# More seven-product pairs in a hybrid attention and SSM block, with weight sums and left factors made ahead

## The chip, the cores and the metric

The kernel runs on one core of one Trainium2 chip. The metric is the device time in microseconds of one execution; lower is better. Every run is a whole execution of the block on its fixed inputs.

## The reference, cut to what matters

One layer takes x (256 rows of 2048) through a norm and one wide product with `w_in`. From that come attention's q, k, v and gate, the SSM's inputs and gate, and two gates of the output. The attention and the SSM results go through one weight matrix each, are gated, added, and go through `w_out`; the input is added and a last norm follows. All is float32.

```
proj = rms_norm(x) @ w_in
q, k, v, z_a, z_s, xbc, dt_raw, g_a, g_s = split(proj)
o_a = attention(q, k, v) * silu(z_a)                 # 16 heads of 128
y = rms_norm(ssd_scan(xbc, dt_raw) * silu(z_s))      # 4096 wide
merged = sigmoid(g_a) * (o_a @ w_attn_branch) + sigmoid(g_s) * (y @ w_ssm_branch)
return rms_norm(x + merged @ w_out)
```

## The kernel before

**Precision.** Each float32 operand of a product is held as two parts, a high part h (type `fp32r`) and a low part l, the rest. ScalarE (ACT) makes h by a copy, VectorE (DVE) makes l by a subtraction. A product is then three matmuls: h with h, h with l, l with h. A "triple" in the code is these three.

**Weights.** All weights lie in one array `wall` of units of 128 x 1024 values (512 KB), in the order in which they are used (`weight_plan`). One unit is loaded by SyncE's DMA queue (SP) into a ring of four buffers w, converted into one of four buffers h and l (`unit`), and used. The conversions are given priority by 120 places (`L_AHEAD`); a scheduler that works with a timeline of its own sets the order of the instructions on every engine, and which of the ring's buffers a load gets.

**Stages**, in order: a first product; the SSM stage, eight groups that project four pairs of xs and zs column blocks each (`project`, `gemm_a`), with convolution, decay, scan and the transposed result `yT` of 32 kt (a kt is 128 rows of the contraction); two pairs ("ssm", 0) and ("ssm", 2) for the SSM branch's 2048 columns; pairs ("v", 0), ("v", 2) and ("ga", 2); attention, 16 heads of q, k and z_a projections with scores, softmax (`scores`), transposed p (`turn_p`) and `mix`; ("ga", 0) and ("ga", 1) by `gates`; the attention branch: pair ("attn", 0), then columns 2 and 3 by `gemm_b`; and pairs ("out", 0), ("out", 2).

**Two ways for a wide product.** `gemm_b` (through `gates`, too) makes 512 columns: per kt and half of the rows one triple, so per two kt and 1024 columns 2 x 2 x 2 x 3 = 24 matmuls of 128x512. `gemm_pair` makes 1024 columns at once. It goes in steps q of two kt. A plain step is again 24 matmuls. A step listed in `S_QUADS` is a quad: the 2 x 2 x 2 block products are made from seven products instead of eight (Strassen's scheme in Winograd's form), so 21 matmuls. A quad needs sums of its four weight blocks and of its four left blocks:

- `t13` and two differences of weights, made by DVE when the weights have come (L432, L437, L438), split into high and low parts `ha, la`, `hc, lc`, and, in two buffers of their own, `ht, lt` and `hu, lu` (L425, L426);
- left factors `sx`, made by `turn_x` from the transposed left matrix: one addition of 128x512 (L355) and four additions or subtractions of 128x128 (L357 to L360), then splits (L230 on ACT, L232 on DVE).

Four extra accumulators `prods` collect products that several outputs share; `fold` adds them at the end.

**Order in time.** Small work is queued with `after(ticks, f)`; a tick is one projection or one step of two kt. `on_unit[n]` runs a function when unit n is converted; `fetch` then lets GpSimd (POOL) copy one column of that unit's h into the target, which makes the DMA behind it wait until then. SP serves its DMAs in their order, and a wait holds up what stands behind it.

Of the kernel before, what the change touches and what calls it, by code (L numbers as in the profile page):

```python
# [15 lines left out]
P = 128  # L16
# [15 lines left out]
MUL_PAD = 112  # L32
# [3 lines left out]
DT_LAG, CB_LAG, TURN_LAG, GT_LAG, Y_LAG, S_LAG, M_LAG = 2, 5, 3, 2, 11, 2, 2  # L36
GS_BEFORE = {0: (0, 1), 4: (2,)}
# [18 lines left out]
def weight_plan():  # L56
# [50 lines left out]
def lay_weights(mats):  # L107
    out = np.empty((N_UNITS, P, UNIT), np.float32)
    for tag, form, src, off, n_kt, w in PLAN:
# [6 lines left out]
        if form == "p":  # L116


            m = m.reshape(n // 2, 2, P, 2, 512)
            for q in range(n // 2):  # L120
                f = FIRST[tag] + 2 * q
                if q in S_QUADS[tag]:
                    out[f] = np.concatenate([m[q, 0, :, 0], m[q, 1, :, 1]], axis=1)
                    out[f + 1] = np.concatenate([m[q, 0, :, 1], m[q, 1, :, 0]], axis=1)
                else:
                    out[f : f + 2] = m[q].reshape(2, P, UNIT)
            continue
# [45 lines left out]
def hybrid_block(ctx: ExitStack, tc: tile.TileContext, wall, xt, x, pk_d, cst_d, fw_d, out):  # L173
# [15 lines left out]
    lead.tile([P, 8], F32, name="fill", tag="fill")  # L189
# [15 lines left out]
    on_unit = {}  # L205

# [6 lines left out]
    def unit(n, shape):  # L213
# [10 lines left out]
        if n in on_unit:  # L224
            on_unit.pop(n)(h[:, 0:1].bitcast(F32))
# [3 lines left out]
    def split(src, hi, lo, scale=1.0):  # L229
        ac.activation(hi, src, AF.Copy, scale=scale)  # L230
        if isinstance(scale, float):
            ve.tensor_tensor(lo, src, hi.bitcast(F32), ALU.subtract)  # L232
        else:
            ve.scalar_tensor_tensor(lo, src, scale, hi.bitcast(F32), ALU.mult, ALU.subtract)

# [35 lines left out]
    def gemm_dt(src):  # L271
# [8 lines left out]
        for u, tag in enumerate("hl"):  # L280
# [4 lines left out]
            if n in on_unit:  # L285
                on_unit.pop(n)(hl[:, 0, 0, 0:1].bitcast(F32))
            ve.tensor_tensor(hl[:, :, 1], w[:, ks], hl[:, :, 0].bitcast(F32), ALU.subtract)
            for kk in range(half_kt):
                kt = u * half_kt + kk
                pe.matmul(  # L290
                    acc, hl[:, kk].rearrange("p n m -> p (n m)"), src[:, kt, :], start=(kt == 0), stop=(kt == KT - 1)
# [6 lines left out]
    def gemm_first(tag, prepare, load_on):  # L298
        name = f"{tag[0]}{tag[1]}"
        accs = [bank("g", 4, f"ps_{name}_{j}") for j in range(4)]  # L300
        for u in range(KT // UB):
# [6 lines left out]
            for kk in range(UB):  # L308
                kt = u * UB + kk
                m = yT[0][:, kt, :]  # L310
# [37 lines left out]
    def turn_x(pool, bufs, temp, x, spare=0):  # L348


        sx = pool.tile([P, 2, 4 - spare, P], F32R, name=f"sx{now[0]}", tag="sx", bufs=bufs)
# [9 lines left out]
        parts = [(sx[:, 0, n], sx[:, 1, n]) for n in range(4 - spare)]  # L361
        if spare:
            own = x[:, 0, P:S], x[:, 0, S + P :]
            split(s[:, 0], *own)
            parts.insert(0, own)
        split(s[:, spare:], sx[:, 0], sx[:, 1])
        return parts

    def gemm_pair(tag, x_of, n_kt, sxs, swap, extra={}, close=1):
# [20 lines left out]
        for q in range(n_q):  # L390
            tick()
            if q in extra:
                extra[q]()
# [3 lines left out]
            if q not in quads:  # L397
                ready = [] if q <= n_q - close else ready
                ready += [(a, k, *unit(n + k, (2, 512))) for k in range(2)]
                if n_q - close <= q < n_q - 1:  # L400
                    continue
                steps = [(e, i, c) for e in ready for i in range(2) for c in range(2)]
                if q == n_q - 1:
                    steps.sort(key=lambda s: s[1:])
                for e, i, c in steps:
# [3 lines left out]
                        start=(q == 0 and k == 0), stop=(q == n_q - 1 and e is ready[-1]),  # L409
# [19 lines left out]
            with tc.high_priority(L_AHEAD):  # L429
                t13 = mul.tile([P, UNIT], F32, name=f"t13_{n}", tag="t13", bufs=1)  # L430
                b12 = wb[:, :512].unsqueeze(1).to_broadcast([P, 2, 512])
                ve.tensor_tensor(two(t13), b12, two(wa), ALU.subtract)  # L432
# [4 lines left out]
                ve.tensor_tensor(wb[:, :512], wa[:, 512:], t13[:, :512], ALU.subtract)  # L437
                ve.tensor_tensor(wb[:, 512:], wb[:, 512:], wb[:, :512], ALU.subtract)  # L438
                ht, lt = hl(mul, "t", ("ht", "lt"), 2)
                part(t13, ht, lt)  # L440
                hu, lu = hl(mul, "u", ("ht", "lt"), 2)
                part(wb, hu, lu)
            sx = sxs[q]
            lo, hi = slice(0, 512), slice(512, 1024)
            go, end = q == quads[0], q == quads[-1]
            for acc, x, h, l, cs, own in (
                (prods[0], a[0][0], ha, la, lo, True),
                (es[1], sx[3], ha, la, hi, False),
                (es[0], a[0][1], hc, lc, lo, False),
                (prods[1], sx[0], ht, lt, lo, True),  # L450
                (prods[3], sx[1], ht, lt, hi, True),
                (prods[2], sx[2], hu, lu, lo, True),
# [16 lines left out]
    def gates(tag, th, src, scales=(0.5, 0.5)):  # L469
        accs = gemm_b(tag, lambda kt: src[:, kt, :])  # L470
# [3 lines left out]
    def rsqrt_rows(sums, n, name):  # L474
# [4 lines left out]
        hr = cpool.tile([P, 2], F32, name=f"hr_{name}", tag="hr", bufs=2)  # L479
# [12 lines left out]
    early = big.tile([P, 29, S], F32, name="early", tag="yo1")  # L492
    xr, dts, rx = early[:, :KT, :], early[:SH, KT:28, :], early[:, 28, :]
    yT = [big.tile([P, KT, 2 * S], F32R, name="yT0", tag="yo0")]
# [15 lines left out]
    def split_x(kt):  # L510
        split(xr[:, kt], yT[0][:, kt, :S], yT[0][:, kt, S:], scale=pk[:, kt : kt + 1])
# [18 lines left out]
    for n in range(4):  # L530
        on_unit[6 + n] = lambda behind, n=n: fetch_x(n, behind)
    on_unit[10] = lambda behind: fetch(cst[:, 1152:], cst_d[:, 1152:], behind)
    on_unit[13] = lambda behind: fetch(cst[:, :1152], cst_d[:, :1152], behind)
# [20 lines left out]
    with tc.tile_pool(name="ssm", bufs=2) as sp:  # L554
# [9 lines left out]
        sp.tile([P, 8], F32, name="line_s", tag="line", bufs=1)  # L564
# [114 lines left out]
        def scan(g, state):  # L679
# [11 lines left out]
            for v, yp in enumerate(yps):  # L691
                u = 2 * g + v
                xs, zs = state["xs"][v], state["zs"][v]
# [9 lines left out]
                if u == 8:  # L703
                    yT.append(big.tile([P, KT, 2 * S], F32R, name="yT1", tag="yo1"))
                dst = yT[u // 8]
                for i in range(2):
                    t = 2 * u + i
                    split(y1[:, i], dst[:, t % 16, :S], dst[:, t % 16, S:], scale=nw[:, t : t + 1])
# [17 lines left out]
        dt_sum(gemm_dt(yT[0]))  # L726
# [18 lines left out]
        for c, u in RX_UNITS.items():  # L745
            on_unit[u] = lambda behind, c=c: (later_rx(c)(behind), norm_x(c))
# [9 lines left out]
        for c in GS_BEFORE[0]:  # L756
            gates(("gs", c), th_s, yT[0], hr_x)

        for g in range(GROUPS):
# [9 lines left out]
            for t in range(max(4 * g, 1), 4 * g + 4):  # L769
# [4 lines left out]
                if t % 4 == 3:  # L774
# [6 lines left out]
                    after(y_lag, lambda a=(g, state): scan(*a), 1)  # L781
                conv(collect(acc, f"x{t}"), t, state["xs"][-1][:, i], f"x{t}")
# [11 lines left out]
    mul.tile([P, MUL_PAD], F32, name="line", tag="line")  # L794
# [13 lines left out]
    def blocks(t, c):  # L808
        return [t[:, i, (c + j) * 512 : (c + j + 1) * 512] for i in range(2) for j in range(2)]

    def two_kts(t, q):
        return t[:, 2 * q : 2 * q + 2, :]

    with tc.tile_pool(name="xp", bufs=1) as xp:
        sxs = {}
        for c in (0, 2):
            for q in S_QUADS[("ssm", c)]:
                if q not in sxs:
                    temp = xp.tile([P, 4, 512], F32, name=f"sxt_y{q}", tag="tmp", bufs=1)
                    sxs[q] = turn_x(xp, 6, temp, two_kts(yT[q // 8], q % 8), 1)  # L820
            es, prods = gemm_pair(
                ("ssm", c), lambda kt: yT[kt // 16][:, kt % 16, :], 2 * KT, sxs, c == 2,
                {2: scale_gate} if c == 0 else {},
# [8 lines left out]
    vth = big.tile([P, 2, 2, D], F32, name="vth", tag="yo1")  # L832
    vt, th_a = vth[:, 0], vth[:, 1]
# [199 lines left out]
```

## Time and profile before

| what | value |
|---|---|
| time, median of 3 runs | 1394.83 us (1394.51 to 1395.12) |
| profiled execution: its span, the one time that its profile gives | 1392.9 us |
| instructions | 19889 |
| TensorE matmuls (PE) | 7308, busy 1381.8 us |
| VectorE (DVE) busy | 1086.8 us |
| ScalarE (ACT) busy | 811.5 us |
| GpSimd (POOL) busy | 32.1 us |
| DMA | 272.33 MB, mean 196 GB/s |

The page of the profile gives for each engine the busy time and its share of the span, then 40 slices of the span (about 35 us each), in which a digit is the busy share in tenths. Other views: groups of instructions (busy time and mean of one in ns, then the idle time of the engine in front of them and who ended it); waits (who waited for whom: us in total, times, longest); windows (busy time of each engine in a stretch, with the count of instructions); and the timeline (start, duration, instruction).

### The profile page before, as it was taken

The page shows a single profiled execution, that of the slowest core. Times are in us where ns is not written, and L with a number is a line of the kernel's source. Part 1 is how long each engine was busy: PE and PEld are TensorE (multiplying, and loading weights), DVE is VectorE, ACT ScalarE, POOL GpSimd, SP SyncE. Part 2 cuts the span into 40 slices and gives each one's busy share as a digit, 9 for nine tenths or more (in the row PEclk, how much of TensorE's full clock was granted, in tenths as well). Part 3 has the DMA queues.
Part 4 walks back from the last instruction along what each step waited for, and adds up shares of the span by engine and source line. Part 5 has one row for each costly group of instructions (what it writes and reads, how often), then busy time and mean ns, then how long its engine had stood idle before and what let it go on. Part 6 is the DMA issues. An engine that isn't in the chain of part 4 may idle for free.

```text
span 1392.9 us, 19889 instructions
## 1 busy us (share of the span) xinstructions
PE 1381.8 (99%) x7308; PEld 1176.8 (84%) x7308; DVE 1086.8 (78%) x1622; ACT 811.5 (58%) x1258; POOL 32.1 (2%) x86
## 2 busy tenths in 40 slices
PE   9999999999999999999999999999999999999997
PEld 7888888888888888888888888888888888888885
DVE  6897887776787787798988988766676666487887
ACT  7656676675667586665554555554554544454454
POOL 1300000000000000000000000000000000000010
PEclk9999999999999999999999999999999999999999
DMA  8766675756566665656666566655555655667564
GB/s 328 243 196 185 197 215 163 221 185 204 172 212 174 208 189 180 194 181 211 192 206 202 187 212 191 217 174 174 168 174 174 181 170 176 199 212 250 172 198 136
DMA packets 78210, 272.33 MB, mean 196 GB/s; under 512 B 8800, under 2 KB 9376, under 8 KB 77728
## 3 DMA queue, kind: packets, MB, share of 16 engines
q1 hardware_dynamic: 77392, 269.88, 61.9%
q8 instruction: 57, 0.93, 0.3%
q10 hardware_dynamic: 720, 1.18, 0.2%
q14 instruction: 41, 0.34, 0.1%
HBM read 268.86 MB, written 2.16 MB: 195 GB/s over the span
## 4 chain that ended last, share of the span: by engine, by line
PE 98%; DVE 1%; DMA 0%; issue 0%; ACT 0%; SPq 0%; POOL 0%; POOLq 0%; DVEq 0%
PE ps_zs L265 8%; PE ps_xs L265 8%; PE ps_zs L268 4%; PE ps_za L265 4%; PE ps_k L265 4%; PE ps_q L265 4%; PE ps_xs L268 4%; PE ps_ssm L384 3%; PE ps_ssm L385 3%; PE ps_ssm L386 3%; PE ps_q L268 2%; PE ps_k L268 2%; PE ps_za L268 2%; PE ps_gs L345 2%; PE ps_gs L343 2%; PE ps_gs L344 2%
## 5 line engine op out<-in xcount | busy, mean ns | idle before, releaser
L223 DVE TENSOR_TENSOR l<-w,h 128x1024 fp32r<-128x1024 f32 (+1 forms) x432 | 522.8, 1213 | 231.0 <-ACT h L222 229.3
L222 ACT ACTIVATE h<-w 128x1024 fp32r<-128x1024 f32 (+1 forms) x432 | 452.8, 1051 | 407.6 <-issue 104.5
L265 PE MATMUL ps_zs<-XT,h 128*128 128x512 f32 x496 | 174.6, 394 | 0.0
L265 PE MATMUL ps_xs<-XT,h 128*128 128x512 f32 x496 | 174.0, 393 | 0.0
L268 PE MATMUL ps_zs<-XT,l 128*128 128x256 f32 x496 | 139.2, 281 | 0.0
L268 PE MATMUL ps_xs<-XT,l 128*128 128x256 f32 x496 | 138.9, 280 | 0.0
L265 PEld LDWEIGHTS ps_zs<-XT,h 128*128 128x128 f32 x496 | 93.0, 187 | 21.3
L265 PEld LDWEIGHTS ps_xs<-XT,h 128*128 128x128 f32 x496 | 92.9, 187 | 20.9
L268 PEld LDWEIGHTS ps_zs<-XT,l 128*128 128x128 f32 x496 | 93.5, 188 | 1.2 <-issue 1.2
L268 PEld LDWEIGHTS ps_xs<-XT,l 128*128 128x128 f32 x496 | 93.5, 189 | 0.0
L265 PE MATMUL ps_q<-XT,h 128*128 128x512 f32 x256 | 92.3, 404 | 0.0
L265 PE MATMUL ps_k<-XT,h 128*128 128x512 f32 x256 | 89.8, 395 | 0.0
L265 PE MATMUL ps_za<-XT,h 128*128 128x512 f32 x256 | 89.7, 394 | 0.0
L268 PE MATMUL ps_q<-XT,l 128*128 128x256 f32 x256 | 71.1, 278 | 0.0
L268 PE MATMUL ps_za<-XT,l 128*128 128x256 f32 x256 | 71.0, 278 | 0.0
L268 PE MATMUL ps_k<-XT,l 128*128 128x256 f32 x256 | 71.0, 277 | 0.0
L385 PE MATMUL ps_ssm<-l,yT 128*128 128x512 f32 x168 | 65.3, 390 | 0.0
L386 PE MATMUL ps_ssm<-h,yT 128*128 128x512 f32 x168 | 65.0, 389 | 0.0
L384 PE MATMUL ps_ssm<-h,yT 128*128 128x512 f32 x168 | 57.5, 390 | 0.0
L265 PEld LDWEIGHTS ps_za<-XT,h 128*128 128x128 f32 x256 | 48.0, 188 | 11.3
L265 PEld LDWEIGHTS ps_k<-XT,h 128*128 128x128 f32 x256 | 48.0, 188 | 11.2
L265 PEld LDWEIGHTS ps_q<-XT,h 128*128 128x128 f32 x256 | 48.1, 188 | 10.9
(520 smaller groups left out, 2984.3 us busy)
## 6 DMA issues: line engine op xcount, KB each, us to landing
w<-in_wall SPq DMA_DIRECT2D x480, 512.0 KB, 3.8
acb<-acum_d SPq DMA_DIRECT2D x32, 256.0 KB, 3.6
th_s<-in_x SPq DMA_DIRECT2D x4, 512.0 KB, 6.5
vth<-in_x SPq DMA_DIRECT2D x1, 2048.0 KB, 9.3
early<-in_xt SPq DMA_DIRECT2D x7, 256.0 KB, 6.9
fw<-in_fw SPq DMA_DIRECT2D x1, 1024.0 KB, 5.5
out<-vth SPq DMA_DIRECT2D x4, 256.0 KB, 2.8
out<-vth ACTq DMA_DIRECT2D x4, 256.0 KB, 3.2
```

The source lines that it names most:

```text
L222: ac.activation(h[:, a:b], w[:, a:b], AF.Copy)
L223: ve.tensor_tensor(l[:, a:b], w[:, a:b], h[:, a:b].bitcast(F32), ALU.subtract)
L265: pe.matmul(acc, h[:, kk, :], m, start=(kt == 0), stop=False)
L268: pe.matmul(acc[:, S:], l[:, kk, :], m[:, :S], start=False, stop=(kt == KT - 1))
L343: pe.matmul(accs[i], xh, h[:, kk], start=(kt == 0), stop=False)
L344: pe.matmul(accs[i], xh, l[:, kk], start=False, stop=False)
L345: pe.matmul(accs[i], xl, h[:, kk], start=False, stop=(kt == KT - 1))
L384: pe.matmul(acc, xh, h, start=start, stop=False)
L385: pe.matmul(acc, xh, l, start=False, stop=False)
L386: pe.matmul(acc, xl, h, start=False, stop=stop)
```

## The change

1. `S_QUADS` has more and other quads: ("ssm", 0) has 5, 7, 8, 10, 11, 13 in place of 5, 7, 9, 11, 13; ("ssm", 2) has the same six in place of 3, 5, 7, 9, 11, 13; ("v", 0) has 2, 4, 6 in place of 4, 6. ("ga", 0) is now a pair of 1024 columns with quads 4, 5, 6, and so is ("attn", 2), with quads 2, 4, 6.
2. For 24 of the 34 quads the two sums of weights are made ahead by `sum_weights`: two loads of weight blocks behind a unit, two subtractions of 128x512 on DVE, and a store to DRAM (`spill`). 11 such jobs lie in the SSM stage, one for every 10 units, and those of ("ga", 0), ("attn", 0), ("attn", 2) and both "out" pairs in the attention stage, one for every 6 units. The quad loads the sum into `wt`, of which there is one buffer, and loads 512 columns less of weights.
3. Left factors of y (six) and of x (four) are made in the SSM stage (`keep_left`), stored to DRAM, and loaded where they are used; ("ga", 0) loads those of x into the unused halves of `hc` and `lc`.
4. The third sum is now one subtraction from both halves of `wa`; which product goes to which accumulator is changed to suit.
5. `yT` and the other large tiles are cut in halves of eight kt, so that their memory is freed in parts. `gemm_pair` takes an order of its steps: ("attn", 2) goes 0, 1, 3, 5, 2, 4, 6, 7 and ("out", 0) goes 0, 1, 2, 4, 3, 6, 5, 7. The last heads' `turn_p` and `mix` are queued sooner. The last reload of x goes in four parts, and `fw` is loaded behind a unit.

```diff
 S_QUADS = {
-    ("ssm", 0): (5, 7, 9, 11, 13), ("ssm", 2): (3, 5, 7, 9, 11, 13),
-    ("v", 0): (4, 6), ("v", 2): (2, 4, 6), ("ga", 2): (2, 4, 6),
-    ("attn", 0): (2, 4, 6), ("out", 0): (3, 5), ("out", 2): (3, 5),
+    ("ssm", 0): (5, 7, 8, 10, 11, 13), ("ssm", 2): (5, 7, 8, 10, 11, 13),
+    ("v", 0): (2, 4, 6), ("v", 2): (2, 4, 6), ("ga", 2): (2, 4, 6),
+    ("ga", 0): (4, 5, 6), ("attn", 0): (2, 4, 6), ("attn", 2): (2, 4, 6), ("out", 0): (3, 5), ("out", 2): (3, 5),
 }
+SX_Y = S_QUADS[("ssm", 0)]
+SX_X = (2, 4, 5, 6)
+SUMS_SSM = [(("ssm", 0), q) for q in (5, 7, 8, 10, 11, 13)] + [(("ssm", 2), q) for q in (7, 10, 13)] + [(("v", 0), 6), (("v", 2), 4)]
+SUMS_ATT = [(t, q) for t in (("ga", 0), ("attn", 0), ("attn", 2), ("out", 0), ("out", 2)) for q in S_QUADS[t]]
+SSM_EVERY, LEFT_EVERY, ATT_EVERY = 10, 11, 6
...
-    for c in range(2):
-        rows(("ga", c), "w_in", OFF_GA + c * 512, KT)
-    pair(("attn", 0), "w_attn_branch", 0, KT)
-    for c in (2, 3):
-        rows(("attn", c), "w_attn_branch", c * 512, KT)
+    pair(("ga", 0), "w_in", OFF_GA, KT)
+    for c in (0, 2):
+        pair(("attn", c), "w_attn_branch", c * 512, KT)
...
+    def spill(kept, key, name, src, shape):
+        kept[key] = dram.tile([P, *shape], F32, name=name, tag=name)
+        nc.sync.dma_start(kept[key], src)
+
+    def sum_weights(tag, q, t, b11, behind):
+        n = FIRST[tag] + 2 * q
+        for dst, src in ((t, wall[n + 1]), (b11, wall[n, :, :512])):
+            gp.tensor_copy(dst[:, 0:1], behind)
+            nc.sync.dma_start(dst, src)
+        ve.tensor_tensor(t[:, :512], t[:, :512], b11, ALU.subtract)
+        ve.tensor_tensor(t[:, 512:], t[:, 512:], t[:, :512], ALU.subtract)
+        spill(presum, (tag, q), f"t_{tag[0]}{tag[1]}_{q}", t, [UNIT])
+
+    def sum_jobs(jobs, begin, every, ts, bs):
+        for n, (tag, q) in enumerate(jobs):
+            a = tag, q, ts[n % len(ts)], bs[n % len(bs)]
+            behind_unit(begin + n * every, lambda behind, a=a: sum_weights(*a, behind))
...
+    def keep_left(key, x, spare, t):
+        sx = t.bitcast(F32R).rearrange("p (e n s) -> p e n s", e=2, n=4)[:, :, spare:]
+        turn_x(sx, t.rearrange("p (n m) -> p n m", n=2), x, spare)
+        spill(lefts, key, f"sxd_{key[0]}{key[1]}", sx.bitcast(F32), [2, 4 - spare, P])
...
+    def fetch_left(pool, bufs, key, x, spare):
+        sx = new_sx(pool, bufs, spare, f"{key[0]}{key[1]}")
+        nc.sync.dma_start(sx.bitcast(F32), lefts[key])
+        return left_parts(sx, x, spare)
...
-            for m in (n, n + 1):
-                if m not in loaded:
-                    load(m)
-            wa, wb = loaded.pop(n), loaded.pop(n + 1)
+            made = (tag, q) in presum
+            wa, wb = ring(f"wa{n}"), ring(f"wb{n}")
+            nc.sync.dma_start(wa, wall[n])
+            if made:
+                wt = mul.tile([P, UNIT], F32, name=f"wt{n}", tag="wt", bufs=1)
+                nc.sync.dma_start(wt, presum[tag, q])
+                nc.sync.dma_start(wb[:, 512:], wall[n + 1, :, 512:])
+            else:
+                wt = wb
+                nc.sync.dma_start(wb, wall[n + 1])
...
-                t13 = mul.tile([P, UNIT], F32, name=f"t13_{n}", tag="t13", bufs=1)
-                b12 = wb[:, :512].unsqueeze(1).to_broadcast([P, 2, 512])
-                ve.tensor_tensor(two(t13), b12, two(wa), ALU.subtract)
+                if not made:
+                    ve.tensor_tensor(wt[:, :512], wt[:, :512], wa[:, :512], ALU.subtract)
                 ha, la = hl(stream, "a", "hl", H_BUFS)
                 part(wa, ha, la)
                 hc, lc = hl(stream, "c", "hl", H_BUFS)
                 part(wb[:, 512:], hc[:, :512], lc[:, :512])
-                ve.tensor_tensor(wb[:, :512], wa[:, 512:], t13[:, :512], ALU.subtract)
-                ve.tensor_tensor(wb[:, 512:], wb[:, 512:], wb[:, :512], ALU.subtract)
+                if not made:
+                    ve.tensor_tensor(wt[:, 512:], wt[:, 512:], wt[:, :512], ALU.subtract)
+                t2 = wt[:, 512:].unsqueeze(1).to_broadcast([P, 2, 512])
+                ve.tensor_tensor(two(wa), two(wa), t2, ALU.subtract)
...
-            sx = sxs[q]
+            if sxs is not None:
+                sx = sxs[q]
+            else:
+                for e, t in enumerate((hc, lc)):
+                    nc.sync.dma_start(t[:, 512:].bitcast(F32), lefts["x", q][:, e].rearrange("p n s -> p (n s)"))
+                sx = [tuple(t[:, 512 + m * P : 512 + (m + 1) * P] for t in (hc, lc)) for m in range(4)]
...
-            after(S_LAG + 6, lambda a=(h, pT, za): mix(*a))
-            after(S_LAG + 3, lambda a=(h, p, pT): turn_p(*a))
+            after(S_LAG + (6, 4, 2)[max(h - 13, 0)], lambda a=(h, pT, za): mix(*a))
+            after(S_LAG + (3 if h < 15 else 1), lambda a=(h, p, pT): turn_p(*a))
...
-        for c in range(2):
-            gates(("ga", c), th_a, XT)
+        es, prods = gemm_pair(("ga", 0), lambda kt: XT[:, kt, :], KT, None, False)
+        open_gate(0, es, prods)
...
-        nc.sync.dma_start(fw, fw_d.partition_broadcast(P))
+        behind_unit(FIRST[("attn", 0)] + 7, lambda behind: fetch(fw, fw_d.partition_broadcast(P), behind))
```

More of the change, by code (lines that the diff above doesn't have):

```diff
@@ L31 @@
 N_WARM = 4
-MUL_PAD = 112
 X_CUTS = ((0, 1), (1, 2), (2, 4), (4, 6), (6, 8), (8, 10))
@@ L389, in gemm_pair @@
         prods = []
-        for q in range(n_q):
+        order = order or range(n_q)
+        seven = [q for q in order if q in quads]
+        for at, q in enumerate(order):
             tick()
-            if q in extra:
-                extra[q]()
+            for f in extra.get(q, ()):
+                f()
             ks = [x_of(2 * q + k) for k in range(2)]
```

228 lines of the change are left out of this document (133 added, 95 removed).

## The prediction

> **What bounds the kernel now.** I read the page first: engine shares, then the slices.
>
> ```profile
> span 1392.9 us, 19889 instructions
> PE 1381.8 (99%) x7308; PEld 1176.8 (84%) x7308; DVE 1086.8 (78%) x1622; ACT 811.5 (58%) x1258; POOL 32.1 (2%) x86
> ...
> DVE  6897887776787787798988988766676666487887
> ...
> GB/s 328 243 196 185 197 215 163 221 185 204 172 212 174 208 189 180 194 181 211 192 206 202 187 212 191 217 174 174 168 174 174 181 170 176 199 212 250 172 198 136
> ```
>
> PE is busy 99% of the span, but a busy PE need not be one at its pace. The Trainium skill says so outright (Perfetto Trace Analysis, Identifying the Most-Contended Engine: matmul busy share does not tell how near the limit a kernel is). So the second view is that of the waits, for PE alone, and the third that of the windows.
>
> ```profile
> engine line waited for: us in total, times, longest us
> PE warm L499 <- DVE ssq L496: 1.4, 1, 1.4
> PE ps_first L313 <- ACT h L222: 0.3, 1, 0.3
> ```
>
> That is the whole answer: PE waits 1.7 us in all, and only at the start.
>
> ```profile
> core 0: us, PE busy (x) PEld busy (x) DVE busy (x) ACT busy (x) POOL busy (x), PEclk, DMA share, GB/s
> 130.00:580.00 450.00, 450.00 (x2672) 388.25 (x2672) 357.08 (x535) 307.65 (x571) 3.88 (x38) 1.00 0.64 194
> 600.00:748.00 148.00, 148.00 (x655) 122.59 (x654) 133.73 (x165) 82.35 (x95) 0.00 (x0) 1.00 0.65 204
> 870.00:1165.00 295.00, 295.00 (x1719) 259.05 (x1718) 194.96 (x374) 147.53 (x227) 0.00 (x0) 1.00 0.59 179
> ```
>
> The windows are the SSM stage, the SSM branch's two pairs, and attention. In the branch every matmul is 128x512; 655 touch 148 us, two of them only with an end: 148/653 = 0.2266 us from start to start. (One matmul shows 0.39 us, because they overlap.) The granted clock is 1.00. So the bound is this pitch times the number of matmuls, almost without a gap, up to the last one:
>
> ```profile
> 1383.31 0.39 PE L386 MATMUL ps_out<-h,mT 128*128 128x512 f32 x1
> ...
> 1387.66 1.00 ACTq L998 DMA_DIRECT2D out<-vth  x2
> ```
>
> Behind it lie 9.6 us to the end of the span: last sums, scaling, stores. DVE is second, 90% busy in the branch (133.73 of 148), where the slices show 8 and 9.
>
> **Part 1, fewer matmuls.** A plain step over two kt is 24 matmuls of 128x512, a seven-product quad 21. The lists grow from 26 to 34 quads: one more in the SSM branch's first half, one in v's first half, three in the gate's first half, three in attention's second half. Nothing else changes on PE: the gate's halves and attention columns were 24 matmuls per two kt before, too, and transposes, scores and mixes stay. 8 x 3 = 24 matmuls x 0.2266 = 5.44 us. All of it is on the path, since PE has no gap that could swallow it. It is also the most that can be won: 1.7 us of waits at the start are not touched, nor is the tail, so I exclude a gain beyond this except for the scatter of the runs (1394.51 to 1395.12).
>
> **Part 2, the work that makes quads.** These are durations by form:
>
> ```profile
> L223 DVE TENSOR_TENSOR l<-w,h 128x1024 fp32r<-128x1024 f32 x424 | 517.5, 1223 | 229.7 <-ACT h L222 228.0
> L432 DVE TENSOR_TENSOR t<-w,w 128x1024 f32<-128x1024 f32 x26 | 31.8, 1225 | 18.6 <-DMA w<-in_wall 18.3
> L426 DVE TENSOR_TENSOR ltt<-t,htt 128x1024 fp32r<-128x1024 f32 x26 | 31.8, 1221 | 0.0
> L438 DVE TENSOR_TENSOR w<-w 128x512 f32<-128x512 f32 x26 | 17.9, 687 | 0.1
> L355 DVE TENSOR_TENSOR sxt_y<-yT 128x512 f32<-128x512 f32 x6 | 4.1, 688 | 0.0
> L357 DVE TENSOR_TENSOR sxt_y<-sxt_y 128x128 f32<-128x128 f32 x6 | 1.7, 290 | 0.0
> L232 DVE TENSOR_TENSOR sx<-sxt_y,sx 128x384 fp32r<-128x384 f32 x6 | 3.3, 555 | 0.0
> L425 ACT ACTIVATE htt<-t 128x1024 fp32r<-128x1024 f32 x26 | 27.6, 1062 | 16.7 <-DVE t L432 16.7
> ```
>
> Sums today cost DVE 1.225 + 2 x 0.687 = 2.6 us per quad. With the sums made ahead a quad keeps one 128x1024 subtraction, 1.2, and 2 x 0.687 = 1.4 us move. The lists name 11 quads for the SSM stage and 13 for attention (3 + 3 + 3 + 2 + 2; the 15 of the heading I can't find). A left factor costs DVE 0.69 + 5 x 0.29 + 0.56 = 2.7 us; six of y and four of x are now made in the SSM stage.
> - SSM stage: 357 + 11 x 1.4 + 10 x 2.7 = 399 of 450 us, 89%.
> - SSM branch: 133.7 - 6 x 2.7 - 9 x 1.4 = 105; the added quad brings 4 x 1.22 + 0.69 = 5.6 in place of two plain conversions of 1.22: 108 of 148, 73%.
> - Attention: 195 + 13 x 1.4 = 213 of 295, 72%.
>
> No stage becomes DVE's, so I cost this at nothing. The cover is the lead of the conversions: DVE stands idle 229.7 us in front of L223, 228.0 of them for ACT's h, which in turn waits for PE to free one of four buffers. They run ahead as far as the buffers let them. If the cover is gone, each lost microsecond is PE's.
>
> **Part 3, DMA.** A job reads 768 KB and writes 512, and its quad later reads 256 more than now: 24 x 1.5 MB = 38 MB, 27 GB/s over the span. In the SSM stage 11 x 1.3 + 4.4 for the left factors is 19 MB, 42 GB/s on top of 194. The first slice moved 328. Bandwidth costs nothing; landing times are what may hurt.
>
> ```profile
> w<-in_wall SPq DMA_DIRECT2D x480, 512.0 KB, 3.8
> acb<-acum_d SPq DMA_DIRECT2D x32, 256.0 KB, 3.6
> ```
>
> **Part 4, quads next to each other.** Until now quads of one pair stand two apart. Now 7, 8 and 10, 11 (SSM branch), 4, 5, 6 (gate) and 2, 4, 6 (attention's second half, where 3 and 5 go first) follow each other. The made sums have one buffer, wt: the next load waits for the last conversion. One link is landing 3.8 + ACT 1.06 + DVE 1.22 = 6.1 us, against 21 x 0.2266 = 4.76 us of PE: 1.3 us short per link, 2.6 for a triple. Two links in the branch and two triples: 7.8 us at most. Against this stands the lead of a quad today, DVE's rows and then PE's use of the same tiles:
>
> ```profile
> 613.45 1.22 DVE L426 TENSOR_TENSOR la<-w,ha 128x1024 fp32r<-128x1024 f32 x1
> 621.85 1.22 DVE L426 TENSOR_TENSOR ltu<-w,htu 128x1024 fp32r<-128x1024 f32 x1
> ...
> 619.61 0.39 PE L385 MATMUL pp_ssm<-la,yT 128*128 128x512 f32 x1
> ...
> 627.54 0.39 PE L385 MATMUL pp_ssm<-ltu,sx 128*128 128x512 f32 x1
> ```
>
> The low parts are ready at 614.67 and 623.07, and used 4.9 and 4.5 us later. That covers 2.6. In the gate one more thing is on the path: left factors of x are loaded into spare halves of the buffers hc and lc, and for quad 6 this load waits for a matmul of quad 4 that stands 22 matmuls ahead of the first use: 22 x 0.2266 = 5.0 us for a 256 KB load, whose nearest row is 3.6. While SP waits for PE there, the next sums and weights of quads 5 and 6 stand behind it, which are due 5 us later or more. A third place is the branch's start: its six left factors can be loaded only when the SSM stage's memory is free, that is, after y's last split, and quad 5's weights and sums stand behind them in SP's queue.
>
> ```profile
> 589.33 0.88 DVE L234 SCALAR_TENSOR_TENSOR yT<-y,pk,yT 128x256 fp32r<-128x256 f32 x2
> ...
> 607.14 0.39 PE L384 MATMUL pp_ssm<-htt,sx 128*128 128x512 f32 x1
> ```
>
> From 590.2 to 607.1 are 16.9 us; 6 x 0.39 + 1.3 = 3.7 MB at 328 GB/s take 11, ACT and DVE 2.3: 3.6 us to spare. Together the bounds are 0 and about 9 us; I take 0.6, near the lower end, because the lead of 4.5 us outweighs each single link.
>
> **Part 5, ends.** Scores to turned p for the last head: now one tick (5.4 us) where it took three; in the built order some 46 matmuls, 10 us, still stand between. The x reload is split in four and fw moves behind a weight unit: late, no one near waits. Costed at nothing.
>
> **Sum.** Span 1392.9 - 5.4 + 0.6 = 1388.1. The median of the runs, 1394.83, stands 1.9 above the profiled span (what lies around it), so the time is **1390.0 us**. A change within 0.2% (2.8 us, between 1392.0 and 1397.6) is about what a measurement of this kernel cannot tell from none.
>
> **Rivals.**
> 1. *The neighbours eat it.* The links of part 4 cost half of their bound, 4 us: 1394.83 - 5.4 + 4 = 1393.4, no change. For it: the lead is that of alternating quads, which is what the change takes away, and DVE's row L432 already waits 18.3 us on loads. Against it: the 4.5 us above. Chance 0.15.
> 2. *Slower: SP's queue.* Each of the 24 jobs puts two loads behind a POOL copy and one store behind DVE's sum into the queue that also carries every weight; what is queued behind a late sum waits with it, and PE waits for that.
>
> ```profile
> SPq L211 <- DVE l L223: 486.1, 227, 8.6
> ```
>
> For it: nearly every weight load leaves SP only when a buffer comes free, so lateness is passed on, and in the SSM stage DVE goes from 79 to 89%. It decides from (5.44 + 2.8)/24 = 0.34 us of PE stall per job; at 0.5 us it is 1389.4 + 12 = 1401.4. The Trainium skill speaks for this rival (DMA: Bandwidth & Descriptors, Anatomy of one DMA: a wait is served by the issuing sequencer before dispatch, not by the DMA engines); the row agrees with that. Against it: the lead of four buffers of 2.7 us each (12 x 0.2266), and the store stands right behind a 1.4 us sum. POOL's copies wait in the same way with the memsets of raw behind them, but POOL is busy 3.9 of 450 us there and raw has three buffers. Chance 0.12.
> 3. *Nothing paced by matmuls.* If something else than the pitch set the time, as the skill's warning allows, fewer matmuls would give 1394.8. PE's 1.7 us of waits speak against it. Chance 0.03.
> That the change doesn't do what it says is excluded: the built program holds 24 matmuls fewer and 34 quads.
>
> **How the numbers follow.** My forecast has 0.70: 1389.0 to 1392.0, with 1390.0 likeliest. Same 0.15 + 0.03 = 0.18, slower 0.12. For 8 in 10 I take the forecast and most of the first rival: 1388.7 to 1396.0.
>
> **What would show it.** In the profile after: matmuls down by 24, PE waits still under some 2 us, the last matmul 9 to 10 us before the end. Right for part 2: DVE near 73% in the branch and 89% before it. Wrong at part 4: rows "PE pp_ga" or "pp_ssm" waiting for DVE lt or ACT ht, or for the DMA into hc and lc. Wrong by rival 2: PE waiting for h or l in the SSM or attention stage, with SP waiting on DVE's sums. A time over 1392 with PE's waits unchanged would overturn the reading of the pitch.

## The result and the profile after

The changed kernel takes **1399.15 us** (median of 7 runs, 1398.23 to 1406.23) against 1394.83 us: ratio 1.004, 95% interval 1.003 to 1.0049. It is slower by 0.4% (0.3% by the two medians alone); the forecast was 1390.0. The profiled execution took 1398.5 us. Lines of its page: the engines, the traffic in 40 slices, the queue that carries the weights, the chain that ended last, and the weight loads:

```profile
span 1396.7 us, 20319 instructions
PE 1382.3 (99%) x7284; PEld 1174.5 (84%) x7284; DVE 1125.5 (81%) x1684; ACT 823.7 (59%) x1279; POOL 75.0 (5%) x143
...
GB/s 321 249 196 216 268 227 245 260 215 278 223 246 207 225 192 213 185 271 246 184 214 248 229 217 172 256 231 256 252 237 243 245 215 174 235 299 179 266 208 139
...
q1 hardware_dynamic: 96032, 318.12, 70.1%
...
PE 87%; DMA 5%; DVE 4%; ACT 2%; issue 1%; POOL 0%; SPq 0%; DVEq 0%; POOLq 0%; ACTq 0%
...
w<-in_wall SPq DMA_DIRECT2D x412, 512.0 KB, 4.5
```

The 24 matmuls are gone, and PE is still busy 99%. But in the chain that ended last (the line that begins with PE 87%) PE no longer holds 98% as before, and DMA and DVE have come into it. The waits of PE and the windows of the three stages:

```profile
PE ps_xs L306 <- DVE l L251: 1.8, 2, 1.3
PE warm L570 <- DVE ssq L567: 1.4, 1, 1.4
PE ps_out L436 <- ACT mT L258: 1.2, 1, 1.2
PE ps_v L436 <- DMA sx_x<-sxd_x: 0.4, 1, 0.4
PE ps_v L437 <- DVE l L251: 0.4, 1, 0.4
PE ps_first L351 <- ACT h L250: 0.2, 1, 0.2
PE ps_k L306 <- DVE l L251: 0.2, 1, 0.2
```

```profile
130.00:580.00 450.00, 448.21 (x2629) 385.72 (x2628) 384.25 (x618) 308.66 (x584) 22.28 (x62) 1.00 0.72 228
600.00:748.00 148.00, 148.00 (x659) 122.64 (x658) 115.16 (x117) 83.18 (x87) 0.70 (x1) 1.00 0.73 236
870.00:1165.00 295.00, 294.82 (x1705) 258.30 (x1704) 209.57 (x400) 148.49 (x228) 15.80 (x26) 1.00 0.73 237
```

PE's waits rise from 1.7 to 5.6 us, and the largest is for a low part l from DVE in the SSM stage. In that stage PE starts 2629 matmuls in the time in which it started 2672 before. DVE is at 384 of 450 us, 85%.

Where the time went is best read from start to start of matmuls at the ends of each stage. Lost is the difference beyond what fewer matmuls give (0.68 us per new quad):

| stretch of PE's stream | before, us | after, us | due | lost, us |
|---|---|---|---|---|
| SSM stage: first ps_B to first ps_ssm | 470.0 | 476.2 | 0 | 6.2 |
| SSM branch: to first ps_v | 167.7 | 167.0 | -0.7 | 0.0 |
| v: to its last matmul | 83.4 | 84.2 | -0.7 | 1.5 |
| gate's second half: to first ps_q | 41.9 | 41.7 | 0 | -0.2 |
| attention, to the last ps_za | 289.7 | 290.1 | 0 | 0.4 |
| gate, attention's branch, output, to the last matmul | 219.9 | 217.8 | -4.1 | 2.0 |

The losses add up to 9.9 us; 0.1 us came back in front of the first ps_B. So 5.4 us were won and 9.8 lost, and the last matmul begins 4.35 us later (first row: the first ps_ssm):

```profile
586.79 0.50 PE L436 MATMUL ps_ssm<-h,yTa 128*128 128x512 f32 x1
...
1387.66 0.39 PE L438 MATMUL ps_out<-h,mT 128*128 128x512 f32 x1
```

The 6.2 us of the SSM stage have three parts. The first is two stalls of 0.65 and 1.5 us beyond the pitch, near 196 and 249 us; with the small losses right beside them they make 2.3 us. The second is scans cut in two: before, the 32 matmuls of a group's scan (yp) always ran together; now the built order puts 2, 10, 8 and 6 of those of four groups some 30 to 50 us ahead of the rest, and yp takes 23.7 us of PE against 22.0. That is 1.7 us. The third, some 2 us, is spread over many starts a few ns longer each; what makes it was not found.

The larger stall, in the timeline (start, duration, engine; in brackets the idle time before and what ended it), in the order SP, ACT, DVE, PE:

```profile
242.59 1.99 SPq L225 DMA_DIRECT2D sums_ssm<-in_wall  x2
...
245.45 1.04 ACT L250 ACTIVATE h<-w 128x1024 fp32r<-128x1024 f32 x1
...
246.24 0.87 DVE L262 SCALAR_TENSOR_TENSOR yTa<-y,pk,yTa 128x256 fp32r<-128x256 f32 x2
248.73 0.69 DVE L226 TENSOR_TENSOR sums_ssm<-sums_ssm 128x512 f32<-128x512 f32 x1 [1.61 <-DMA sums_ssm<-in_wall]
249.34 1.22 DVE L251 TENSOR_TENSOR l<-w,h 128x1024 fp32r<-128x1024 f32 x1
...
250.61 0.39 PE L306 MATMUL ps_xs<-XT,l 128*128 128x256 f32 x1 [1.30 <-DVE l L251]
```

ACT has h ready at 246.49 and DVE is free at 247.1. But next in DVE's order stands a sum whose load has not landed. DVE stands 1.61 us, makes the sum, and only then the l that PE stands for. Grouped, DVE's rows L226 (first of the two subtractions) and its conversions:

```profile
L251 DVE TENSOR_TENSOR l<-w,h 128x1024 fp32r<-128x1024 f32 x408 | 495.3, 1220 | 118.6 <-ACT h L250 117.3
...
L226 DVE TENSOR_TENSOR th_a<-th_a 128x512 f32<-128x512 f32 x13 | 9.0, 692 | 38.9 <-DMA th_a<-in_wall 38.9
...
L226 DVE TENSOR_TENSOR sums_ssm<-sums_ssm 128x512 f32<-128x512 f32 x11 | 7.6, 692 | 20.8 <-DMA sums_ssm<-in_wall 20.8
```

Every job costs DVE its 1.4 us of work and a stand at the landing: 1.9 us each in the SSM stage, 3.0 in attention. The stands are 59.7 us in all. The idle time in front of the conversions has fallen from 229.7 to 118.6 us.

### The profile page after: what moved, and what is told of

The parts are those of the page before. It is cut to its first block, busy times and chain, and to the rows that moved or that the text cites. A ratio compares the mean times of both kernels' runs of the same rounds, so it can differ in the third digit from the quotient of the medians.

```text
span 1396.7 us, 20319 instructions
## 1 busy us (share of the span) xinstructions
PE 1382.3 (99%) x7284; PEld 1174.5 (84%) x7284; DVE 1125.5 (81%) x1684; ACT 823.7 (59%) x1279; POOL 75.0 (5%) x143
## 4 chain that ended last, share of the span: by engine, by line
PE 87%; DMA 5%; DVE 4%; ACT 2%; issue 1%; POOL 0%; SPq 0%; DVEq 0%; POOLq 0%; ACTq 0%
PE ps_zs L303 7%; PE ps_xs L303 7%; PE ps_za L303 4%; PE ps_k L303 4%; PE ps_q L303 4%; PE ps_zs L306 4%; PE ps_xs L306 4%; PE ps_ssm L436 3%; PE ps_ssm L437 3%; PE ps_ssm L438 3%; DMA w<-in_wall 2%; PE ps_k L306 2%; PE ps_za L306 2%; PE ps_gs L383 2%; PE ps_gs L382 2%; PE ps_gs L381 2%
## 5 line engine op out<-in xcount | busy, mean ns | idle before, releaser
L250 ACT ACTIVATE h<-w 128x1024 fp32r<-128x1024 f32 (+1 forms) x416 | 433.9, 1048 | 328.6 <-issue 59.1
L251 DVE TENSOR_TENSOR l<-w,h 128x1024 fp32r<-128x1024 f32 (+1 forms) x416 | 500.6, 1210 | 120.5 <-ACT h L250 119.1
L303 PE MATMUL ps_xs<-XT,h 128*128 128x512 f32 x496 | 175.2, 394 | 0.0
L721 ACT ACTIVATE gt<-acb,acT 128x128 f32<-128x128 f32 x128 | 43.9, 390 | 31.5 <-DMA acb<-acum_d 27.8
L486 DVE TENSOR_TENSOR la<-wa,ha 128x1024 fp32r<-128x1024 f32 x34 | 41.5, 1222 | 19.8 <-ACT ha L485 19.5
L485 ACT ACTIVATE ha<-wa 128x1024 fp32r<-128x1024 f32 x34 | 36.0, 1058 | 35.1 <-DMA wa<-in_wall 24.8
```

Source lines behind the costliest of these rows:

```text
L250: ac.activation(h[:, a:b], w[:, a:b], AF.Copy)
L251: ve.tensor_tensor(l[:, a:b], w[:, a:b], h[:, a:b].bitcast(F32), ALU.subtract)
L303: pe.matmul(acc, h[:, kk, :], m, start=(kt == 0), stop=False)
L485: ac.activation(h, src, AF.Copy)
L486: ve.tensor_tensor(l, src, h.bitcast(F32), ALU.subtract)
L721: ac.activation(g4[:, n, b], acb[:, j, b // 2 * P : b // 2 * P + P], AF.Relu, scale=-1.0, bias=sc[:, h : h + 1],)
```

## The experiments

Theories: A, DVE pays (standing at the loads and doing the sums, in the queue that also holds the conversions). B, SP's queue pays (the prediction's second rival). C, the left factors or the new layout pay. All kernels, with the ratio to the kernel before and the SSM stage (first ps_B to first ps_ssm, one profile each):

| kernel | us, median | ratio, 95% | SSM stage, us |
|---|---|---|---|
| before | 1394.9 | | 470.0 |
| changed | 1399.15 | 1.004 (1.003 to 1.0049) | 476.2 |
| no sums in SSM | 1403.04 | 1.0055 (1.0039 to 1.0072) | 471.8 |
| no sums in attention | 1423.06 | 1.0194 (1.0167 to 1.0222) | 480.8 |
| sums late | 1397.93 | 1.0025 (1.0016 to 1.0035) | 474.1 |
| POOL's sums | 1395.77 | 1.0002 (0.9992 to 1.0011) | 472.3 |
| sums left out | 1393.43 | 0.9988 (0.9978 to 0.9997) | 471.8 |
| standing only | 1396.58 | 1.0007 (0.9998 to 1.0015) | 472.7 |
| work only | 1396.22 | 1.0009 (1.0 to 1.0017) | 473.7 |
| POOL's sums, left factors late | 1393.48 | 0.9989 (0.998 to 0.9999) | 470.5 |
| POOL's sums, output in order | 1396.57 | 1.0011 (1.0001 to 1.002) | 472.9 |
| POOL's sums and queue | 1394.56 | 1.0 (0.999 to 1.001) | 471.9 |
| the same, y's left factors late | 1393.14 | 0.9988 (0.9979 to 0.9997) | 470.7 |
| **POOL's sums, y's left factors late** | **1392.12** | **0.998 (0.9971 to 0.9989)** | **470.5** |
| attention half only | 1396.91 | 1.0017 (1.0008 to 1.0027) | 470.5 |
| the same, POOL's sums | 1397.77 | 1.0018 (1.0009 to 1.0027) | 470.5 |

One caution for the last column: "no sums in attention" has, in its SSM stage, the same instructions in the same order on every engine as the changed kernel, and shows 480.8 against 476.2. In its profile PE stood 2.9 us at the place of the larger stall (1.3 in the changed kernel), and the granted clock then was 0.50 for 3.4 us. Where DVE is behind, one profile of a stage is uncertain by some us. The profiled runs also lie up to 2.8 us from the median of their kernel. So medians carry the verdicts.

**No sums in SSM** (`SUMS_SSM = []`).

> The eleven sum jobs of the SSM stage are left out; their quads make their own sums. Everything else is the changed kernel. Theory A (DVE stands in its own queue at the landing of the sums' loads, 20.8 us in the SSM stage of the changed kernel, and so loses the lead of its conversions): the SSM stage ends near 582 us instead of 586.6, the two PE waits of 0.9 and 1.7 us at 196 and 249 us are gone; the branch and v, whose quads stand next to each other, give back 0 to 3 us; 1394 to 1398 us. Theory B (SP's queue: loads behind POOL's copies and stores behind DVE's sums delay the weights behind them): the same here, so this run does not tell A from B, it tells both from Theory C (the ten left factors, or the memory's new layout, cost the time): then the SSM stage stays at 585 us or later and the time at 1398 to 1401.

The SSM stage recovers to 471.8, so C is out for most of the loss. The time, though, missed the expectation by 5 us: the branch takes 175.2 us instead of 167.0. These are PE's waits in it:

```profile
PE ps_ssm L436 <- ACT h L250: 1.8, 3, 0.6
...
PE pp_ssm L437 <- DVE ltt L486: 1.1, 1, 1.1
...
PE pp_ssm L436 <- ACT htt L485: 0.6, 1, 0.6
```

Neighbouring quads that make their own sums did not keep PE's pace here; so making the sums ahead is worth more than it costs, and what costs is where they are made.

**No sums in attention** (`SUMS_ATT = []`).

> The thirteen sum jobs of the attention stage are left out; the quads of the gate, of attention's branch and of the output make their own sums. Attention itself lost only about 0.5 us in the changed kernel although DVE stood 38.9 us at these loads, so by theories A and B it gains 0.5 us at most there. A quad that makes its own sums takes DVE 4 x 1.22 + 2 x 0.69 + 0.69 = 7 us against 4.76 us of PE, so three in a row (gate, attention's second half) fall behind by up to 2 x 2.2 us each: 1398 to 1408 us. If it is below 1397, the jobs of attention cost more than the trace shows as gaps.

Far above: 1423. Quads that make their own sums are short again: the gate's first half, attention's branch and the output take some 6 us more each than in the changed kernel (45.4, 91.2 and 97.2 against 39.6, 85.4 and 91.2). The longest single wait is in the output, for mT; the second row is the stand in the SSM stage:

```profile
PE ps_out L436 <- ACT mT L258: 7.4, 1, 7.4
PE ps_xs L306 <- DVE l L251: 3.8, 2, 2.9
PE pp_attn L436 <- ACT htt L485: 1.5, 3, 0.7
```

The windows of the same profile show what followed the stand of 2.9 us, which ended at 254.7: the column before the last two is the granted clock.

```profile
250.00:256.00 6.00, 3.06 (x18) 2.37 (x17) 3.35 (x5) 2.65 (x5) 0.00 (x0) 1.00 0.45 159
256.00:259.40 3.40, 3.40 (x14) 2.92 (x13) 2.94 (x6) 3.40 (x9) 0.00 (x0) 0.50 0.80 216
```

The same was seen for 3.4 us at 1300.5, behind four waits in 6 us (the longest 0.9), and for 6.9 us at 1338.0, in the wait of 7.4. So a stand of PE can cost more than its own length; the stands of 1.2 to 1.3 us in the changed kernel were not followed by it.

**Sums late.** Loads behind unit n as before, the sums behind unit n + 4 (SSM) or n + 3 (attention):

```diff
+        gp.tensor_tensor(nil, behind, behind, ALU.subtract)
+        gp.tensor_tensor(b11[:, 0:1], b11[:, 0:1], nil, ALU.add)
         ve.tensor_tensor(t[:, :512], t[:, :512], b11, ALU.subtract)
```

> Loads, stores and sums all stay, but each sum is tied to a weight unit four units (SSM) or three (attention) behind its loads, by two small POOL operations that write one column of the operand back unchanged, so that DVE meets a load that has landed. Theory A: DVE's waits for these loads fall from 59.7 us to under 10, the SSM stage ends near 582 to 584 us, and the time is 1393.5 to 1396.5. Theory B: the loads and stores stand in SP's queue as before, the stores behind sums that come later: no gain, 1398 to 1401, with SP waiting for sums as long as before or longer. Theory C: no change, 1398 to 1400.

DVE's stands at the loads are gone (only 4.3 us at POOL's operations in attention stay), but only 1.2 us were won by the medians, and the intervals overlap. Standing is not the whole of A.

**POOL's sums** (`ve.tensor_tensor` to `gp.tensor_tensor` in both lines of sum_weights).

> The two subtractions of each of the 24 sum jobs run on POOL instead of DVE; loads and stores stay on SP. POOL then stands at the loads, not DVE. Theory A: DVE's waits for these loads are gone and its 34 us of sums too, the SSM stage ends near 581 to 583 us, time 1392 to 1396, unless POOL's two subtractions take so long that raw's small memsets come late. Theory B: stores wait for sums that are slower than DVE's: 1399 to 1404. Theory C: no change.

3.4 us less than the changed kernel, at the upper end of what A expected, and against B, since the stores now wait for slower sums:

```profile
L227 POOL TENSOR_TENSOR th_a<-th_a 128x512 f32<-128x512 f32 x13 | 24.6, 1893 | 1.0
L226 POOL TENSOR_TENSOR sums_ssm<-sums_ssm 128x512 f32<-128x512 f32 x11 | 19.7, 1792 | 54.2 <-DMA sums_ssm<-in_wall 54.2
```

POOL stands 54.2 us at the loads of the SSM stage, and no compute engine waits for these sums. SP does, with the stores behind them: 40.0 us in the SSM stage and 50.7 in attention.

**Sums left out, standing only, work only.** Three kernels that split A; none of them makes the sums that the quads read. The first leaves out both subtractions; the second has one of 128x4 in their place; the third makes both ahead of the loads, on what the buffers held (the cut below shows the first two):

```diff
-        ve.tensor_tensor(t[:, :512], t[:, :512], b11, ALU.subtract)
-        ve.tensor_tensor(t[:, 512:], t[:, 512:], t[:, :512], ALU.subtract)
+        ve.tensor_tensor(t[:, :4], t[:, :4], b11[:, :4], ALU.subtract)   # second kernel only
```

> The changed kernel with the two subtractions of each of the 24 sum jobs left out; the loads, POOL's copies and the stores stay, so SP's queue and the DMA traffic are the same, and a store now waits for the landing itself instead of for DVE. It tells DVE (A) from SP's queue and traffic (B). A: DVE neither stands at the loads nor sums, the SSM stage ends near 582 us as with POOL's sums, and the time is 1393 to 1397. B: SP stands at every store for a landing of 4 to 5 us with weights behind it, the SSM stage ends at 586 or later, 1398 to 1406.

> The changed kernel with each job's two subtractions of 128x512 cut to one of 128x4, at the same place in DVE's order: DVE still stands at the landing of the loads, but does next to no work there (the sums that the quads read are not made). If standing is the cost: DVE's waits for the loads stay at 55 to 60 us, the SSM stage ends at 585 or later, 1396.5 to 1399. If the 34 us of DVE's work are the cost: 582 to 583, 1393.5 to 1395. Leaving both out gave 1393.4, both together 1399.2.

> The changed kernel with each job's two subtractions made ahead of its loads, on what the buffers held, so that DVE does the same work and does not stand at a landing (the sums that the quads read are not made). Loads and stores stay in SP's queue; two memsets of POOL are added. If standing is the cost: 1393.5 to 1395, SSM stage at 582 to 583. If DVE's work is the cost: 1396.5 to 1399, SSM stage at 585 or later. If both give about half, each of the two runs lies near 1396.

Both together 1399.2, standing alone 1396.6, work alone 1396.2, neither 1393.4: by the medians each costs about 3 us, and they add. That both together cost 5.7 us is clear of the scatter; the size of each part is not, since the runs of these two kernels spread over 4.5 and 6.3 us and their intervals barely clear that of the first. DVE's waits in the second kernel show that it did stand as long as in the changed one:

```profile
DVE th_a L226 <- DMA th_a<-in_wall: 42.0, 13, 4.2
...
DVE sums_ssm L226 <- DMA sums_ssm<-in_wall: 17.4, 10, 2.7
```

B falls with the first kernel. Its loads and stores are those of the changed kernel, and now SP itself stands at the landings, with the stores; its waits, SP's row and then PE's:

```profile
SPq L218 <- DMA th_a<-in_wall: 38.9, 13, 4.0
...
PE warm L568 <- DVE ssq L565: 1.4, 1, 1.4
PE ps_v L434 <- DMA sx_x<-sxd_x: 0.3, 1, 0.3
PE ps_attn L434 <- ACT h L248: 0.3, 1, 0.3
```

PE never waits for a conversion in the SSM stage. The scans changed, too: yp takes 22.6 us with the sums left out or standing only, 23.0 with work only and 23.65 in the changed kernel. So some 1.1 of the 5.7 us are scans that the built order cuts in two when DVE has these sums to make.

**POOL's sums, left factors late.** The ten left factors made where the kernel before makes them:

```diff
-        for n, q in enumerate(SX_X):
-            behind_unit(begin + 3 + n * LEFT_EVERY, lambda behind, q=q: left_x(q, behind))
...
+            for q in ((5,) if c else (2, 4, 6)):   # at the head of each half of v
...
+                sx_of_x[q] = turn_x(sx, temp, two_kts(XT, q))
```

> POOL makes the sums, as in the run before, and the ten left factors are no longer made in the SSM stage but at the head of the SSM branch (six of y) and of v (three, and one before its second half), as the kernel before does; those of x are stored for the gate from there. Theory: the left factors' 2.7 us each of DVE are what is left of the SSM stage's loss (582.4 against 580.5 before): it ends at 580.5 to 581.5. In return DVE has 6 x 2.7 us more at the head of the branch and 3 x 2.7 at the head of v, where plain conversions run ahead: 0 to 3 us there. 1393 to 1397. Rival: what is left in the SSM stage is not DVE's work but small losses of pitch, and the stage stays at 582.

As expected: the stage is at 470.5, all scans in one piece (yp 22.0 us). v takes 86.0 us against 83.5 with POOL's sums alone.

**POOL's sums, output in order** (order `None` for the output's first half).

> POOL makes the sums, and the first half of the output takes its pairs of kt in their natural order (0 to 7) instead of 0, 1, 2, 4, 3, 6, 5, 7. The wait of 0.9 to 1.5 us in front of the fourth pair (for the turned columns of attention's second half, kt 8 and 9) should go, since pair 3 needs columns that are there long before: 0.6 to 1.5 us less than with POOL's sums alone, 1394 to 1395.5. Rival: quad 3's left factors and conversions, due one pair earlier, are late in its place, and nothing is won: 1395.5 to 1397.

Nothing won, as the rival said: from the first ps_out to the last matmul it is 90.6 us, with the other order 90.7. The wait for mT is gone from PE's waits, and smaller losses of 0.1 to 0.3 us stand in its place.

**POOL's queue**, alone and with y's left factors late; and the latter with SP's queue.

```diff
-            nc.sync.dma_start(dst, src)
+            gp.dma_start(dst, src)
```

> POOL makes the sums and also issues the jobs' loads and stores from its own queue, so that SP's queue carries none of them. Theory B (SP's queue): the loads and stores behind POOL's copies and sums still cost something with POOL's sums (SP stands 40 us at sums_ssm, 51 at th_a, 32 at POOL's copies): without them the SSM stage ends near 581 and the time falls to 1392 to 1394.5. Theory A (DVE was all of it): no difference to POOL's sums with SP's queue, 1395 to 1396.5, or slower where POOL's descriptors take its time from raw's memsets.

> POOL makes the sums and issues their loads and stores; the six left factors of y are made at the head of the SSM branch again, where they cost nothing measurable in the run with late left factors (branch 167.1 us, as in the changed kernel), and the four of x stay in the SSM stage, since made at the head of v they cost 2.6 us there. Theory A: the SSM stage ends near 581.5, v takes 83.4, and with the 5.4 us of the eight quads the time is 1391.5 to 1393.5, below the kernel before by more than 0.1%. Rival: the pieces do not add up (runs of each scatter by 2 to 4 us), 1393.5 to 1395.

> The same, with the sums' loads and stores in SP's queue. If SP's queue costs about 1 us (1394.6 against 1395.8 in the two runs with POOL's sums), it is 1392.5 to 1394.5, about 1 us above the kernel with POOL's queue; if SP's queue is innocent, the two are equal.

SP's queue costs nothing that can be told: 1392.1 us with it and 1393.1 without in the last two kernels, 1395.8 with it and 1394.6 without where y's left factors are made early, and the intervals of each pair overlap. The last of the three is the best version, 0.2% faster than the kernel before. Its waits:

```profile
PE warm L570 <- DVE ssq L567: 1.4, 1, 1.4
PE ps_first L351 <- ACT h L250: 0.8, 2, 0.6
PE ps_v L437 <- DVE l L251: 0.7, 1, 0.7
PE ps_out L436 <- ACT mT L258: 0.6, 1, 0.6
PE ps_k L306 <- DVE l L251: 0.5, 1, 0.5
```

No wait is left in the SSM stage. v, k and the output still wait.

**The attention half alone.** Six new quads, the SSM branch's and v's lists as before, x's left factors at the head of v; sums by DVE, then by POOL.

> Only the attention half of the change: six more quads (three in the gate's first half, three in attention's second half), the 13 sums for them and for the output made in attention by DVE; no sum and no left factor in the SSM stage, and the lists of the SSM branch and of v as in the kernel before (26 + 6 = 32 quads). If the SSM stage paid all of the loss: its end is back at 580.7, attention costs 0.5 us, 6 x 0.68 = 4.1 us are won, 1390.8 to 1392.5. If the losses in front of v, k and the output come with the change as such (new memory, the order of the output, DVE's standing of 39 us in attention): 1392.5 to 1395.

> The same with POOL making the sums of attention. DVE stands 39 us at the loads there in the changed kernel with 213 us of work in 295, and PE lost only about 0.5 us: POOL can win at most that, 1390.3 to 1392, or it is equal.

Both missed. The SSM stage is as good as back (470.5), but the time is 1397. In the first one's profile v takes 86.5 us against 83.4 (left factors at its head, which are also stored there), the branch 168.8 against 167.7, PE waits 1.4 us for h at the start, 0.3 at k and 1.0 at the output. In the second one's profile PE waits 2.3 us for h at the start, the granted clock is 0.50 from 12.0 to 15.4 us, and the first ps_B comes 2.6 us later than before. So this pair does not show the six quads by themselves, what they are worth alone stays open, and the SSM stage is not the only payer.

## Why the prediction was wrong, step by step

**What bounds the kernel** was right as far as it went: with DVE out of the way the quads do win, and the branch, with one quad more, is 0.7 us shorter, as the pitch of 0.2266 us says. But "PE waits 1.7 us in all" was taken as the measure of all losses. After the change PE lost 9.8 us, and its waits grew by 3.9 alone (from 1.7 to 5.6). Scans in two pieces and longer starts are no waits.

**Part 1** held: 24 matmuls, 5.44 us. "Nothing else changes on PE" did not. The planner that places work by its own clock moved parts of four scans, 1.7 us: 1.1 of them go with DVE's sums in the SSM stage, the other 0.6 with y's left factors, since yp takes 22.6 us without the former and 22.0 with the latter made late as well. The built order shows such a move before any run; the working above looked in it for matmuls that go, not for those that change place.

**Part 2 is the step that failed.** I counted DVE's busy time (399 of 450 us forecast, 384 measured) and costed it at nothing, because conversions had 229.7 us of idle time in front of them. Two errors lie in that. A sum behind a load was priced as 1.4 us; on DVE's queue it is 1.4 plus the stand, 3.3 us in the SSM stage and 4.4 in attention. And idle time in front of conversions is not a cover that can be spent anywhere: it is a lead of at most four buffers, and it is gone at single places (249 us) while the stage's mean, busy and standing together (384 + 20 of 450 us, 90%), still shows room. The means themselves were near: 78% and 71% in the branch and attention, 73 and 72 forecast. Left factors of y cost another 1.3 us there (471.8 without DVE's sums, 470.5 without y's left factors too); those of x nothing measurable.

**Part 3** held: 34 GB/s more in the SSM stage (194 to 228, where 42 were forecast), w's landing 3.8 to 4.5 us, and the kernel with the sums left out has all these transfers and is still faster than the kernel before, at 1393.4.

**Part 4** held for the links: no wait in the branch, and 0.2 us in the gate. I took 0.6. (Its bound counted two links in the branch. Both halves have the pairs 7, 8 and 10, 11, so there are four, and 7.8 us should have been 10.4.) That the made sums are what covers the neighbours was not weighed; without them the branch takes 8.2 us more. The three places that I looked at were the wrong ones. v's own head, where left factors of x are loaded just ahead of their use (0.4 us at sx_x, 0.4 at l), lost 1.5 us in all.

**Part 5, "costed at nothing"**, failed by 1.5 us: the fourth pair of the output stands in front of mT of attention's second half (1.2 us by the waits, 1.5 from start to start). This and a small stand at k are in most kernels that keep the change's attention half, 0.2 to 1.2 us by the waits, in the best version 0.6 and 0.5. With the sums left out and with both kinds of left factors late neither shows, and the output then takes 90.0 and 89.8 us against 91.2. With its pairs in order it takes 90.6 without any wait for mT, so that wait is not shown to be the whole cause. Why the stands differ so from profile to profile was not settled.

**Rivals.** The second had the sign and almost the time (1401.4) by the wrong mechanism. SP's queue costs nothing that these runs can tell. The rival asked for 0.34 us per job; DVE's sums cost 5.7 us, 0.24 per job (1399.15 against 1393.43 with the sums left out). The other 4.0 us, from 1389.4 to 1393.43, are not tied down so well. The profile of the kernel without the sums, a run of 1391.7 us, lost 1.8 us in the SSM stage (1.3 of them go with y's left factors), 0.5 in v, 0.3 in attention and 0.9 behind it. So v's and the output's 1.5 us in the changed kernel are in part the sums' as well. The rival's sign, "PE waiting for h or l in the SSM or attention stage, with SP waiting on DVE's sums", was seen too: in the SSM stage SP waits 12.5 us for sums_ssm, with the stores. Such a sign tells the two apart only if one of them is taken away, as by leaving the sums out. The Trainium skill's sentence on queues (DMA: Bandwidth & Descriptors, Anatomy of one DMA: the issuing sequencer serves a wait before dispatch) agrees with the trace, in which SP stood 38.9 us at th_a with the sums left out, but it spoke for the wrong queue here: the stand that cost time was in the consumer's queue.

**The size.** The best version lies 2.1 us above the forecast. Its profile, a run of 1392.4 us, lost 1.3 us in v (84.0 against 82.7), 1.3 from the gate's first half to the last matmul, 0.7 in attention, 0.6 in the SSM stage and 0.4 in the branch, 4.3 in all. Of these 0.6 were in the forecast, and 1.0 came back at the start, in the gate's second half and behind the last matmul. That leaves 2.7, about the 2.4 us by which this run lies above the forecast.

## What to carry to other kernels

Price an operation moved into an engine's gaps with its stand at the load in front of it, since an in-order engine that stands holds everything behind it; and look for the place where several such pieces meet, not at the stage's mean. Give such work to an engine that no compute engine waits for, even a slower one; here POOL's sums won 3.4 us. If the result is a sign that two mechanisms share, take one of them away.

## What the runs showed of the hardware

POOL's subtraction of 128x512 took 1.4 to 1.9 us on the mean of its groups (1.3 at the least) where DVE's takes 0.69, and while POOL made sums DVE's 128x256 convolution step in the SSM stage rose from 0.483 to 0.529 us, so POOL's help is not quite free. POOL's copy of a single column, 128x1, is shown with 0.85 us on the mean in the SSM stage against 0.10 for a memset of 128x4 (spans on POOL are rough). A scan's 32 matmuls run in 2.75 us in one piece; cut into 2 and 30, or 10 and 22, the pieces add up to 3.32, into 8 and 24 to 2.90, into 6 and 26 to 3.10. A stand of PE of 2.9 us was followed by a granted clock of 0.50 for 3.4 us (no sums in attention); one of 1.3 us was not (the changed kernel).
